# Prompt scores of a decoder step: two stacked full-height maps, or two maps in the two row halves

## The chip, the core and the metric

The program runs on one core of a Trainium2 chip. TensorE multiplies (PE; its weight loads are shown as PEld and run beside the products), VectorE (DVE), ScalarE (ACT) and GpSimd (POOL) do the elementwise work, SyncE (SP) issues the DMAs. The metric is the device time of one execution in microseconds (us), as the median of several runs.

## What is computed

One step of a hybrid decoder layer, for a prompt of 1024 tokens and 8 sample tokens, model width 1024. One projection of h feeds differential attention (4 heads, two maps of 64 channels each, values of 128), a short gated convolution and a chunk-mixing branch; the branches are projected, gated, merged, projected again and normalised. The change concerns the prompt's attention alone:

```python
def block(args):                      # 128 queries at a time
    q_blk, i = args
    s = jnp.einsum('bqhmd,bkhmd->bhmqk', q_blk, k).astype(jnp.float32) * ATT_SCALE
    q_pos = i * Q_BLOCK + jnp.arange(Q_BLOCK)
    mask = key_pos[None, :] <= q_pos[:, None]
    p = jax.nn.softmax(jnp.where(mask, s, -jnp.inf), axis=-1)
    a = p[:, :, 0] - lam * p[:, :, 1]
    return jnp.einsum('bhqk,bkhd->bqhd', a.astype(v.dtype), v)
```

m is the map: each head has two score matrices, each a product over 64 channels.

## The kernel before

Activations lie transposed, channels on the 128 partitions and 1032 tokens along the rows. Every large product is made of exact parts: an operand is split into a rounded part hi (float32r) and a rest lo (`split`, line 85: ACT copies hi, DVE or POOL subtracts), and `gemm` (line 235) adds hi·hi, hi·lo and lo·hi into one PSUM tile `ps_z` of 344 columns: eight chunks of 128 channels, so 24 products for each of the three units of tokens. The program is written in a fixed order. Twice in a unit, after 12 of its 24 products and at its end, `gemm` calls `tick` (line 101), which lets every active side stream (a Python generator) emit its next piece. Each engine runs its instructions in the order in which they were emitted.

The prompt attention of a head is such a side stream (`attention`, line 384). Its plan (lines 496 to 512) gives the tick of each step: block i of 128 queries starts at `start[i]`, scores of map 0 at that tick, of map 1 at the next, then `scale`, `combine`, the transposes and `av`. One head's attention is thus spread over ticks that lie between projection products of the next chunks (`conv_chunk`, the next head's Q, K, V).

For the scores, `evac_q` (line 332) and `evac_k` (line 349) prepare stacked operands of 128 rows. Q0 holds map 0's queries as hi in rows 0 to 63 and lo in rows 64 to 127, Q1 the same for map 1 with hi below. KA holds K's hi part twice, KB its lo part twice, one pair for each map. Two products of full height, KA and KB against the same Q, then give (hi + lo)·(hi + lo) of one map (`scores_map`, lines 429 and 430). The block's keys are nk = 128 (i + 1) columns; from 640 on they are cut into two slices of nk/2. DVE adds the mask and takes the row maximum out of PSUM (line 432), then ACT takes the exponential (line 437). Score tiles come from the pool PX of five PSUM tiles (`xtile`), `ps_z` and `av` from PZ, which has three.

Of the kernel before, what the change touches and what calls it, by code (L numbers as in the profile page):

```python
# [8 lines left out]
F32 = mybir.dt.float32  # L9
F32R = mybir.dt.float32r  # L10
I32 = mybir.dt.int32
AF = mybir.ActivationFunctionType
ALU = mybir.AluOpType
# [3 lines left out]
P = 128  # L17
D = 1024
KD = D // P
NP = 1024  # L20
# [10 lines left out]
SCALE = DK ** -0.5  # L31
# [33 lines left out]
def step_kernel(ctx, tc, cT, sm, sn, lamb, xT, x_p, x_s, ada, adag, bgate, w_in, w_br, w_out, lnb,  # L65
# [12 lines left out]
    S = Slots(spool, NS)  # L78

    pe, act, dve, pool, sp = nc.tensor, nc.scalar, nc.vector, nc.gpsimd, nc.sync  # L80

    def mm(out, lhsT, rhs, start, stop, **kw):
        pe.matmul(out, lhsT=lhsT, rhs=rhs, start=start, stop=stop, **kw)  # L83

    def split(hi, lo, src, eng=None):
        act.copy(hi, src)  # L86
        (eng or dve).tensor_tensor(lo, src, hi, ALU.subtract)  # L87
# [4 lines left out]
    def xtile(name, shape=(P, 512)):  # L92
        return px.tile(list(shape), F32, tag="x", name=name)

    def mtile(name, w):
        return mpool.tile([P, w], F32, tag=f"m{w}", name=name, bufs=12 if w == 2 else 4 if w < 16 else 2)
# [51 lines left out]
    vS = cpool.tile([P, H, NB], F32, name="vS")  # L148
    pt = cpool.tile([1, NB * PAGES], I32, name="pt")

# [1 line left out]
    wseq = []  # L152

    def want(kind, c):
# [22 lines left out]
    first = {c: [S.new(f"w0{x}{c}", F32R) for x in "hl"] for c in (C_Q, C_K, C_V)}  # L177
# [73 lines left out]
                w_split()  # L251
            tick()

# [1 line left out]
    xk, adr = {}, {}  # L255

    def load_ada(k):
# [68 lines left out]
        hh.append(a)  # L326
        hl.append(b)

# [1 line left out]
    st = {}  # L330

    def evac_q(h):
        q0 = S.new(f"Q0_{h}", F32R)
        q1 = S.new(f"Q1_{h}", F32R)
        st["Q", h] = (q0, q1)

        def f(u, a, b, ps):
            b2 = min(b, NP)
            n = b2 - a
            if n:  # L340
                act.copy(q0[0:64, a:b2], ps[0:64, :n])
                dve.tensor_tensor(q0[64:128, a:b2], ps[0:64, :n], q0[0:64, a:b2], ALU.subtract)
                act.copy(q1[64:128, a:b2], ps[64:128, :n])
                dve.tensor_tensor(q1[0:64, a:b2], ps[64:128, :n], q1[64:128, a:b2], ALU.subtract)
            if u == 2:
                dve.tensor_copy(qS[:, h, :], ps[:, n:n + NB])
        return f

    def evac_k(h):
        kf = S.new(f"kf{h}")  # L350

        def f(u, a, b, ps):
            act.copy(kf[:, a:b], ps)
            if u < 2:
                return
            later.append(lambda: sp.dma_start(out=kT_o[h], in_=kf))
            ka0, ka1, kb0, kb1 = (S.new(f"{n}_{h}", F32R) for n in ("KA0", "KA1", "KB0", "KB1"))
            st["K", h] = (ka0, ka1, kb0, kb1)
            pool.tensor_copy(kS[:, h, :], kf[:, NP:T])
            f0, f1 = kf[0:64, :NP], kf[64:128, :NP]  # L360
            dve.tensor_copy(ka0[0:64, :NP], f0)
            act.copy(ka0[64:128, :NP], f0)
            dve.tensor_tensor(kb0[0:64, :NP], f0, ka0[0:64, :NP], ALU.subtract)
            act.copy(kb0[64:128, :NP], kb0[0:64, :NP].bitcast(F32))
            dve.tensor_copy(ka1[64:128, :NP], f1)
            act.copy(ka1[0:64, :NP], f1)
            dve.tensor_tensor(kb1[64:128, :NP], f1, ka1[64:128, :NP], ALU.subtract)
            act.copy(kb1[0:64, :NP], kb1[64:128, :NP].bitcast(F32))
            S.free()
        return f  # L370

# [12 lines left out]
    def attention(h):  # L384
# [6 lines left out]
        mask = S.new(f"mask{h}")  # L391
# [3 lines left out]
        Q, K = st["Q", h], st["K", h]  # L395
        oacc[h] = S.new(f"o{h}")
        E, aT, V = {}, {}, {}

        tmp = {}

        def scores(i, m):
            nk = (i + 1) * P
            if m:
                e, mx, nb, su, rc = tmp.pop(i)
                scores_map(i, 1, nk, e, mx, nb, su)
                tmp[i] = (e, su, rc)
                if i == 7:
                    S.free(7)
                return
            if nk <= 512:  # L410
                t = S.new(f"E{h}_{i}", F32, (P, 2, 512))
                e = [t[:, 0, :nk], t[:, 1, :nk]]
            else:
                e = [S.new(f"E{h}_{i}_{m}")[:, :nk] for m in range(2)]
            mx = mtile(f"mx{h}_{i}", 4)
            nb = mtile(f"nb{h}_{i}", 2)
            su = mtile(f"su{h}_{i}", 2)
            rc = mtile(f"rc{h}_{i}", 2)
            tmp[i] = (e, mx, nb, su, rc)
            scores_map(i, 0, nk, e, mx, nb, su)  # L420

        def scores_map(i, m, nk, e, mx, nb, su):
            g = 1 if nk <= 512 else 2
            w = nk // g
            qq = Q[m][:, i * P:(i + 1) * P]
            for j in range(g):
                ps = xtile(f"s{h}_{i}_{m}_{j}")
                c = slice(j * w, (j + 1) * w)
                mm(ps[:, :w], qq, K[m][:, c], True, False)
                mm(ps[:, :w], qq, K[2 + m][:, c], False, True)  # L430
                m0 = 1024 - nk + j * w
                dve.tensor_tensor_reduce(
                    e[m][:, c], ps[:, :w], mask[:, m0:m0 + w], 1.0,
                    mx[:, 2 * m:2 * m + 1] if j else -3.0e38, ALU.add, ALU.max,
                    mx[:, 2 * m + j:2 * m + j + 1])
            dve.tensor_scalar(nb[:, m:m + 1], mx[:, 2 * m + g - 1:2 * m + g], -SCALE, None, ALU.mult)  # L436
            act.activation(e[m], e[m], AF.Exp, bias=nb[:, m:m + 1], scale=SCALE,  # L437
                           accum_out=su[:, m:m + 1])

        def scale(i):  # L440
            e, su, rc = tmp[i]
# [62 lines left out]
        for i, t in enumerate(start):  # L504
            at(t, scores, i, 0)
            at(t + 1, scores, i, 1)
            at(t + 2, scale, i)
            at(t + 3, combine, i)
            at(t + (7 if i > 2 else 6), trans, i, 0)
            if i >= 4:  # L510
                at(t + 8, trans, i, 1)
# [5 lines left out]
            yield  # L517
        S.free(2)

# [1 line left out]
    yb = {}  # L521

    def conv_chunk(h):
# [47 lines left out]
        gemm("z", C_GC + h, hh, hl, e_gc)  # L571
        gemm("z", C_CB + h, hh, hl, e_cb)

# [1 line left out]
    lt = S.new("lt")  # L575

    def startup():
# [41 lines left out]
        for i, c in enumerate(cs):  # L619
            for k in range(KD):  # L620
                for x, w in enumerate(first[c]):
                    mm(small[0:16, i * P:(i + 1) * P], hs[:, 16 * k:16 * k + 16],
                       w[:, k * P:(k + 1) * P], k == 0 and x == 0, k == KD - 1 and x == 1,
                       skip_group_check=True)
        evs = [f(0) for f in (evac_q, evac_k, evac_v)]
        for c, f in zip(cs, evs):
            for u, (a, b) in enumerate(cut):
# [27 lines left out]
        dve.tensor_scalar(gsub, c2("subg"), 1.0 - LAM0, None, ALU.mult)  # L655
        S.free()

# [1 line left out]
    dec = {}  # L659
    vmax = [0]  # L660

# [185 lines left out]
    for h in range(H):  # L847
        if h:
            gemm("z", C_Q + h, hh, hl, evac_q(h))
            gemm("z", C_K + h, hh, hl, evac_k(h))  # L850
        active.append(attention(h))
        if h == H - 1:
            dec_g = decode(active[0])
            active.append(dec_g)
        if h:
            gemm("z", C_V + h, hh, hl, evac_v(h))
        conv_chunk(h)
    later.append(lambda: sp.dma_start(out=conv_o, in_=convo))

# [1 line left out]
    merged = {}  # L861

    def branch_parts(n, res, gap=0):
# [45 lines left out]
    lo_eng[0] = dve  # L909
    merge(1, True)  # L910

# [1 line left out]
    cvT = {}  # L913

    def evac_cv(g):
# [132 lines left out]

    merge(2, False)

# [1 line left out]
    sq = []  # L1052
    row = mpool.tile([P, H + 1 + NB], F32R, tag="row", name="row", bufs=1)
    dve.tensor_copy(row[:, 0:H], ident[:, 0:P:32])
# [110 lines left out]
    S.free(16)  # L1165
    drain(ag)

# [1 line left out]

    mh, ml = {}, {}  # L1170
    for d in range(KD):
# [41 lines left out]
    for i, n in enumerate(order):  # L1213
# [3 lines left out]
        r = S.new(f"r{n}")  # L1217
# [3 lines left out]
        for f, (a, b) in enumerate(zip(cuts, cuts[1:])):  # L1221
            ps = pz.tile([P, 512], F32, tag="z", name=f"out{n}_{f}")[:, :b - a]
            c = slice(a, b)
            rc = r[0:rows, c]
# [25 lines left out]
        if last:  # L1250
            nb = sd[0:rows, 1:2]
            dve.scalar_tensor_tensor(nb, mu, -1.0, rstd, ALU.mult, ALU.mult)
            rc = r[:, 720:1024]
# [3 lines left out]
        for a, b in ((0, 360), (360, 720)) if last else ((0, 512), (512, 1024)):  # L1257
            rc = r[0:rows, a:b]
# [98 lines left out]
```

## Time and profile before

| what | value |
|---|---|
| runs | 1199.52 us median of 3 (1199.45 to 1200.81) |
| profiled execution, from first to last instruction | span 1197.8 us |
| PE busy | 1180.9 us, 99% of the span |
| DVE, ACT, POOL busy | 640.4, 356.3, 381.8 us |
| granted TensorE clock, mean | 0.998 |

The profile gives no other time of the profiled execution than its span; it is one execution, and the runs are others of the same program. Busy times of different engines overlap. A matmul's length in the profile includes the way through the array, so lengths of successive products overlap as well, and the distance from one start to the next says more than a length.

### The profile page before, as it was taken

To read this page: it belongs to the slowest core of one execution; us is meant where nothing else is said; L and a number is where in the kernel's file an instruction comes from. 1 tells how busy PE (TensorE), PEld (TensorE's weight loads), DVE (VectorE), ACT (ScalarE), POOL (GpSimd) and SP (SyncE) were. 2 spreads that over 40 slices of the span, in tenths; PEclk is the share of its full clock that TensorE was granted. 3 is DMA by queue.
4 is the path that set the end of the run, shared out by engine and by line. 5 is a ranking of instruction groups with operands and counts; after the bars stand their busy time and mean duration, and the time that the engine had idled before them with its cause. 6 is when DMAs were issued, how large, how long until landed. Compare 5 with 4: busy or idle time off the path is not lost.

```text
span 1197.8 us, 20253 instructions
## 1 busy us (share of the span) xinstructions
PE 1180.9 (99%) x7599; PEld 1097.3 (92%) x7599; DVE 640.4 (53%) x1190; ACT 356.3 (30%) x709; POOL 381.8 (32%) x304
## 2 busy tenths in 40 slices
PE   7999999999999999999999999999999999999997
PEld 5799999999999999999999999888887899997785
DVE  5656547536625655777776775111211451197766
ACT  3344454343444342121224223111012232343000
POOL 2123222322322406999980001211211222254000
PEclk9999999999999999999999999999999999999999
DMA  9411110111111116777852234666674111133231
GB/s 358 184 63 37 49 59 29 43 71 37 36 53 63 36 46 208 248 249 234 259 186 65 75 106 140 230 216 223 215 244 158 54 44 45 46 119 120 89 106 53
DMA packets 73300, 146.62 MB, mean 122 GB/s; under 512 B 8409, under 2 KB 9306, under 8 KB 73202
## 3 DMA queue, kind: packets, MB, share of 16 engines
q1 hardware_dynamic: 73202, 145.34, 36.3%
q8 instruction: 59, 0.97, 0.3%
q14 instruction: 39, 0.32, 0.1%
HBM read 136.80 MB, written 8.51 MB: 121 GB/s over the span
## 4 chain that ended last, share of the span: by engine, by line
PE 95%; DVE 3%; DMA 1%; issue 0%; SPq 0%; POOL 0%; ACT 0%
PE ps_z L83 62%; PE ps_b L83 8%; PE out L83 8%; PE acc L83 3%; PE s L83 3%; PE dacc L83 3%; PE av L83 2%; PE t L461 1%; DVE wol L87 1%; DVE ml L1178 1%; DMA ada<-in_ada 1%; PE pa L83 1%; DVE wl L87 1%; PE mix L83 1%; PE cvt L952 0%
## 5 line engine op out<-in xcount | busy, mean ns | idle before, releaser
L83 PE MATMUL ps_z<-hh,wh 128*128 128x344 f32 x1560 | 509.3, 326 | 0.0
L83 PE MATMUL ps_z<-hh,wl 128*128 128x344 f32 x1560 | 498.8, 320 | 0.0
L83 PE MATMUL ps_z<-hl,wh 128*128 128x344 f32 x1560 | 498.3, 319 | 0.0
L83 PEld LDWEIGHTS ps_z<-hh,wh 128*128 128x128 f32 x1560 | 293.3, 188 | 25.8 <-issue 20.2
L83 PEld LDWEIGHTS ps_z<-hl,wh 128*128 128x128 f32 x1560 | 293.6, 188 | 1.5 <-issue 0.2
L83 PEld LDWEIGHTS ps_z<-hh,wl 128*128 128x128 f32 x1560 | 293.1, 188 | 0.2 <-DVE wl L87 0.2
L87 POOL TENSOR_TENSOR wl<-wr,wh 128x512 fp32r<-128x512 f32 x72 | 99.3, 1381 | 265.4 <-ACT wh L86 236.2
L723 POOL TENSOR_TENSOR kp<-kp,QB 128x1024 f32<-128x1024 f32 x64 | 162.0, 2563 | 12.3 <-DMA kp<-in_cache_k 11.4
L87 DVE TENSOR_TENSOR wl<-wr,wh 128x512 fp32r<-128x512 f32 x82 | 85.6, 1044 | 50.3 <-ACT wh L86 44.8
L710 DVE TENSOR_REDUCE Sdec<-kp 128x16 f32<-128x1024 f32 x64 | 77.4, 1213 | 37.8 <-POOL kp L723 37.8
L885 POOL TENSOR_TENSOR mg<-mg,sg 128x344 f32<-128x344 f32 x24 | 28.3, 1180 | 213.6 <-DVE sg L884 213.6
L83 PE MATMUL ps_b<-yh,wh 128*128 128x344 f32 x288 | 94.3, 328 | 0.4
L86 ACT CAST wh<-wr 128x512 fp32r<-128x512 f32 x154 | 93.2, 615 | 0.2
L83 PE MATMUL ps_b<-yl,wh 128*128 128x344 f32 x288 | 92.1, 320 | 0.0
L83 PE MATMUL ps_b<-yh,wl 128*128 128x344 f32 x288 | 92.1, 320 | 0.0
L901 ACT ACTIVATE sg<-ps_z 128x344 f32<-128x344 f32 x48 | 22.0, 458 | 213.3 <-PE ps_z L83 193.3
L437 ACT ACTIVATE E<-E,nb 128x128 f32<-128x128 f32 (+7 forms) x64 | 49.8, 777 | 112.3 <-DVE nb L436 107.0
L83 PEld LDWEIGHTS ps_b<-yh,wh 128*128 128x128 f32 x288 | 54.1, 188 | 11.5 <-issue 5.2
L884 DVE SCALAR_TENSOR_TENSOR sg<-sg,ps_b 128x344 f32<-128x344 f32 x24 | 12.3, 513 | 92.3 <-PE ps_b L83 89.1
L83 PEld LDWEIGHTS ps_b<-yl,wh 128*128 128x128 f32 x288 | 54.2, 188 | 0.1
L83 PEld LDWEIGHTS ps_b<-yh,wl 128*128 128x128 f32 x288 | 54.2, 188 | 0.0
L83 PE MATMUL out<-woh,ml 128*128 128x512 f32 (+1 forms) x136 | 51.9, 382 | 0.0
(285 smaller groups left out, 1518.2 us busy)
## 6 DMA issues: line engine op xcount, KB each, us to landing
wr<-in_w_in SPq DMA_DIRECT2D x136, 256.0 KB, 2.7
kp<-in_cache_k SPq DMA_DIRECT2D x128, 256.0 KB, 3.5
vp<-in_cache_v SPq DMA_DIRECT2D x128, 256.0 KB, 3.6
ada<-in_ada SPq DMA_DIRECT2D x16, 512.0 KB, 8.1
wr<-in_w_br SPq DMA_DIRECT2D x24, 256.0 KB, 2.6
xT<-in_xT SPq DMA_DIRECT2D x8, 516.0 KB, 9.7
adag<-in_adag SPq DMA_DIRECT2D x8, 512.0 KB, 5.7
wr<-in_w_out SPq DMA_DIRECT2D x16, 256.0 KB, 2.6
```

Of the source, the lines that this page charges most:

```text
L83: pe.matmul(out, lhsT=lhsT, rhs=rhs, start=start, stop=stop, **kw)
L86: act.copy(hi, src)
L87: (eng or dve).tensor_tensor(lo, src, hi, ALU.subtract)
L437: act.activation(e[m], e[m], AF.Exp, bias=nb[:, m:m + 1], scale=SCALE, accum_out=su[:, m:m + 1])
L461: pe.transpose(ps[:, kb - lo, :], E[i][:, kb * P:(kb + 1) * P], ident)
L710: dve.reduce_sum(Sx[:, b, 2 * j:2 * j + 2, :], tiles.pop(i).rearrange("p e (a d) -> p e a d", d=DK), axis=AX.X)
L723: pool.tensor_tensor(t, t, q, ALU.mult)
L884: dve.scalar_tensor_tensor(sg[u], sg[u], 1.0, ps, ALU.add, ALU.mult)
L885: pool.tensor_tensor(merged[d][:, a:b], merged[d][:, a:b], sg[u], ALU.add)
L901: act.activation(sg[u], ps, AF.Tanh, scale=0.5)
L1178: dve.scalar_tensor_tensor(ml[d][:, a:b], m, 0.5, mh[d][:, a:b].bitcast(F32), ALU.mult, ALU.subtract)
```

## The change

`evac_q` and `evac_k` no longer stack: for each head there is one pair Qh, Ql and one pair Kh, Kl, 128 rows each, where rows 0 to 63 are map 0 and rows 64 to 127 map 1. `scores(i, j)` now does column slice j of both maps: for each map three products of 64 rows, hi·hi, lo·hi and hi·lo (lo·lo is left out), map 0 in the upper rows of the array and map 1 in the lower, alternating, each map into a PSUM tile of its own. Blocks 0 to 3 have one slice and emit everything at their first tick; blocks 4 to 7 emit slice 0 of both maps at the first tick and slice 1, with both exponentials, at the second. The two K tiles that fall away give two buffers of the pool S back.

```diff
@@ -326,22 +326,19 @@
     st = {}
 
     def evac_q(h):
-        q0 = S.new(f"Q0_{h}", F32R)
-        q1 = S.new(f"Q1_{h}", F32R)
-        st["Q", h] = (q0, q1)
+        qh = S.new(f"Qh_{h}", F32R)
+        ql = S.new(f"Ql_{h}", F32R)
+        st["Q", h] = (qh, ql)
 
         def f(u, a, b, ps):
             b2 = min(b, NP)
             n = b2 - a
             if n:
-                act.copy(q0[0:64, a:b2], ps[0:64, :n])
-                dve.tensor_tensor(q0[64:128, a:b2], ps[0:64, :n], q0[0:64, a:b2], ALU.subtract)
-                act.copy(q1[64:128, a:b2], ps[64:128, :n])
-                dve.tensor_tensor(q1[0:64, a:b2], ps[64:128, :n], q1[64:128, a:b2], ALU.subtract)
+                split(qh[:, a:b2], ql[:, a:b2], ps[:, :n])
             if u == 2:
                 dve.tensor_copy(qS[:, h, :], ps[:, n:n + NB])
         return f
@@ -354,18 +351,10 @@
             if u < 2:
                 return
             later.append(lambda: sp.dma_start(out=kT_o[h], in_=kf))
-            ka0, ka1, kb0, kb1 = (S.new(f"{n}_{h}", F32R) for n in ("KA0", "KA1", "KB0", "KB1"))
-            st["K", h] = (ka0, ka1, kb0, kb1)
+            kh, kl = S.new(f"Kh_{h}", F32R), S.new(f"Kl_{h}", F32R)
+            st["K", h] = (kh, kl)
             pool.tensor_copy(kS[:, h, :], kf[:, NP:T])
-            f0, f1 = kf[0:64, :NP], kf[64:128, :NP]
-            dve.tensor_copy(ka0[0:64, :NP], f0)
-            act.copy(ka0[64:128, :NP], f0)
-            dve.tensor_tensor(kb0[0:64, :NP], f0, ka0[0:64, :NP], ALU.subtract)
-            act.copy(kb0[64:128, :NP], kb0[0:64, :NP].bitcast(F32))
-            dve.tensor_copy(ka1[64:128, :NP], f1)
-            act.copy(ka1[0:64, :NP], f1)
-            dve.tensor_tensor(kb1[64:128, :NP], f1, ka1[64:128, :NP], ALU.subtract)
-            act.copy(kb1[0:64, :NP], kb1[64:128, :NP].bitcast(F32))
+            split(kh[:, :NP], kl[:, :NP], kf[:, :NP])
             S.free()
         return f
 
@@ -398,44 +387,41 @@
 
         tmp = {}
 
-        def scores(i, m):
+        def scores(i, j):
             nk = (i + 1) * P
-            if m:
-                e, mx, nb, su, rc = tmp.pop(i)
-                scores_map(i, 1, nk, e, mx, nb, su)
+            g = 1 if nk <= 512 else 2
+            w = nk // g
+            if j == 0:
+                if g == 1:
+                    t = S.new(f"E{h}_{i}", F32, (P, 2, 512))
+                    e = [t[:, 0, :nk], t[:, 1, :nk]]
+                else:
+                    e = [S.new(f"E{h}_{i}_{m}")[:, :nk] for m in range(2)]
+                tmp[i] = (e, mtile(f"mx{h}_{i}", 4), mtile(f"nb{h}_{i}", 2), mtile(f"su{h}_{i}", 2),
+                          mtile(f"rc{h}_{i}", 2))
+            if j >= g:
+                return
+            e, mx, nb, su, rc = tmp[i]
+            c = slice(j * w, (j + 1) * w)
+            ps = [xtile(f"s{h}_{i}_{m}_{j}") for m in range(2)]
+            for x, y in ((0, 0), (0, 1), (1, 0)):
+                for m in range(2):
+                    r = slice(64 * m, 64 * m + 64)
+                    mm(ps[m][:, :w], Q[x][r, i * P:(i + 1) * P], K[y][r, c], x + y == 0, x == 1)
+            m0 = 1024 - nk + j * w
+            for m in range(2):
+                dve.tensor_tensor_reduce(
+                    e[m][:, c], ps[m][:, :w], mask[:, m0:m0 + w], 1.0,
+                    mx[:, 2 * m:2 * m + 1] if j else -3.0e38, ALU.add, ALU.max,
+                    mx[:, 2 * m + j:2 * m + j + 1])
+                if j == g - 1:
+                    dve.tensor_scalar(nb[:, m:m + 1], mx[:, 2 * m + j:2 * m + j + 1], -SCALE, None, ALU.mult)
+                    act.activation(e[m], e[m], AF.Exp, bias=nb[:, m:m + 1], scale=SCALE,
+                                   accum_out=su[:, m:m + 1])
+            if j == g - 1:
                 tmp[i] = (e, su, rc)
                 if i == 7:
-                    S.free(7)
-                return
-            if nk <= 512:
-                t = S.new(f"E{h}_{i}", F32, (P, 2, 512))
-                e = [t[:, 0, :nk], t[:, 1, :nk]]
-            else:
-                e = [S.new(f"E{h}_{i}_{m}")[:, :nk] for m in range(2)]
-            mx = mtile(f"mx{h}_{i}", 4)
-            nb = mtile(f"nb{h}_{i}", 2)
-            su = mtile(f"su{h}_{i}", 2)
-            rc = mtile(f"rc{h}_{i}", 2)
-            tmp[i] = (e, mx, nb, su, rc)
-            scores_map(i, 0, nk, e, mx, nb, su)
-
-        def scores_map(i, m, nk, e, mx, nb, su):
-            g = 1 if nk <= 512 else 2
-            w = nk // g
-            qq = Q[m][:, i * P:(i + 1) * P]
-            for j in range(g):
-                ps = xtile(f"s{h}_{i}_{m}_{j}")
-                c = slice(j * w, (j + 1) * w)
-                mm(ps[:, :w], qq, K[m][:, c], True, False)
-                mm(ps[:, :w], qq, K[2 + m][:, c], False, True)
-                m0 = 1024 - nk + j * w
-                dve.tensor_tensor_reduce(
-                    e[m][:, c], ps[:, :w], mask[:, m0:m0 + w], 1.0,
-                    mx[:, 2 * m:2 * m + 1] if j else -3.0e38, ALU.add, ALU.max,
-                    mx[:, 2 * m + j:2 * m + j + 1])
-            dve.tensor_scalar(nb[:, m:m + 1], mx[:, 2 * m + g - 1:2 * m + g], -SCALE, None, ALU.mult)
-            act.activation(e[m], e[m], AF.Exp, bias=nb[:, m:m + 1], scale=SCALE,
-                           accum_out=su[:, m:m + 1])
+                    S.free(5)
 
         def scale(i):
             e, su, rc = tmp[i]
```

The rest of the diff takes out comment lines.

On PE, head 0, block 0, of the kernel before (s_0_0 and s_0_1 are the score tiles of map 0 and 1, ps_z a projection; 12 products of it stand between the two ticks):

```order
L83 MATMUL ps_z_2_829<-hh_606,wl_516 128x344
L83 MATMUL s_0_0_0_867<-KA_0_776,Q_0_719 128x128
L83 MATMUL s_0_0_0_867<-KB_0_778,Q_0_719 128x128
L83 MATMUL ps_z_0_873<-hh_172,wh_647 128x344
...
L83 MATMUL ps_z_0_873<-hh_359,wl_648 128x344
L83 MATMUL s_0_1_0_886<-KA_0_777,Q_0_720 128x128
L83 MATMUL s_0_1_0_886<-KB_0_779,Q_0_720 128x128
L83 MATMUL ps_z_0_873<-hh_426,wh_764 128x344
```

The same place after:

```order
L83 MATMUL ps_z_2_817<-hh_606,wl_516 128x344
L83 MATMUL s_0_0_0_855<-Kh_772,Qh_719 128x128
L83 MATMUL s_0_1_0_856<-Kh_772,Qh_719 128x128
L83 MATMUL s_0_0_0_855<-Kl_773,Qh_719 128x128
L83 MATMUL s_0_1_0_856<-Kl_773,Qh_719 128x128
L83 MATMUL s_0_0_0_855<-Kh_772,Ql_720 128x128
L83 MATMUL s_0_1_0_856<-Kh_772,Ql_720 128x128
L83 MATMUL ps_z_0_869<-hh_172,wh_647 128x344
```

Map 1 has moved up to map 0's tick, and four products of 128 rows in two pairs have become six of 64 rows in one run, map 0 and map 1 by turns.

On PE, head 0, block 4, before (the last number of a name but one is the slice):

```order
L83 MATMUL ps_z_2_1157<-hh_359,wl_909 128x344
L83 MATMUL s_4_0_0_1176<-KA_0_776,Q_0_719 128x320
L83 MATMUL s_4_0_0_1176<-KB_0_778,Q_0_719 128x320
L83 MATMUL s_4_0_1_1180<-KA_0_776,Q_0_719 128x320
L83 MATMUL s_4_0_1_1180<-KB_0_778,Q_0_719 128x320
L83 MATMUL ps_z_2_1157<-hh_426,wh_964 128x344
...
L83 MATMUL ps_z_2_1157<-hh_606,wl_965 128x344
L83 MATMUL s_4_1_0_1202<-KA_0_777,Q_0_720 128x320
L83 MATMUL s_4_1_0_1202<-KB_0_779,Q_0_720 128x320
L83 MATMUL s_4_1_1_1206<-KA_0_777,Q_0_720 128x320
L83 MATMUL s_4_1_1_1206<-KB_0_779,Q_0_720 128x320
L83 MATMUL ps_z_0_1212<-hh_172,wh_1085 128x344
```

And after, where the third part shows the start of the second tick's run:

```order
L83 MATMUL ps_z_2_1153<-hh_359,wl_899 128x344
L83 MATMUL s_4_0_0_1172<-Kh_772,Qh_719 128x320
L83 MATMUL s_4_1_0_1173<-Kh_772,Qh_719 128x320
L83 MATMUL s_4_0_0_1172<-Kl_773,Qh_719 128x320
L83 MATMUL s_4_1_0_1173<-Kl_773,Qh_719 128x320
L83 MATMUL s_4_0_0_1172<-Kh_772,Ql_720 128x320
L83 MATMUL s_4_1_0_1173<-Kh_772,Ql_720 128x320
L83 MATMUL ps_z_2_1153<-hh_426,wh_956 128x344
...
L83 MATMUL ps_z_2_1153<-hh_606,wl_957 128x344
L83 MATMUL s_4_0_1_1198<-Kh_772,Qh_719 128x320
L83 MATMUL s_4_1_1_1199<-Kh_772,Qh_719 128x320
```

Each tick of block 4 had both slices of one map in four products; it now has one slice of both maps in six.

## Rows read from the trace of the kernel before

**Rows 1.** The page: span, PE's busy time and share, the chain by engine and line

```profile
span 1197.8 us, 20253 instructions
...
PE 1180.9 (99%) x7599; PEld 1097.3 (92%) x7599; DVE 640.4 (53%) x1190; ACT 356.3 (30%) x709; POOL 381.8 (32%) x304
...
PE 95%; DVE 3%; DMA 1%; issue 0%; SPq 0%; POOL 0%; ACT 0%
PE ps_z L83 62%; PE ps_b L83 8%; PE out L83 8%; PE acc L83 3%; PE s L83 3%; PE dacc L83 3%; PE av L83 2%; PE t L461 1%; DVE wol L87 1%; DVE ml L1178 1%; DMA ada<-in_ada 1%; PE pa L83 1%; DVE wl L87 1%; PE mix L83 1%; PE cvt L952 0%
```

**Rows 2.** Busy time by stretches: us, then PE, PEld, DVE, ACT, POOL, clock, DMA

```profile
75.00:175.00 100.00, 100.00 (x661) 98.98 (x660) 57.12 (x159) 46.25 (x105) 30.89 (x34) 1.00 0.14 48
175.00:275.00 100.00, 100.00 (x659) 99.11 (x658) 50.93 (x130) 42.12 (x90) 29.88 (x31) 1.00 0.14 48
```

**Rows 3.** All waits of PE: us in total, times, longest

```profile
PE pa L83 <- DMA ada<-in_ada: 6.9, 3, 5.9
PE pb L83 <- ACT part L300: 0.5, 1, 0.5
```

**Rows 4.** Chain from 70 to 425 us by line; groups of instructions, the scores

```profile
by line: PE ps_z L83 78.4%; PE s L83 9.6%; PE av L83 6.9%; PE t L461 4.1%; PE vt L476 1.0%
...
L83 PE MATMUL s<-KA,Q 128*128 128x384 f32 (+5 forms) x96 | 32.9, 344 | 0.0
```

**Rows 5.** Pieces of the chain in order of time: start, us, what

```profile
78.27 0.23 PE s L83 x2
...
78.51 1.88 PE ps_z L83 x12
...
172.23 0.47 PE s L83 x2
...
181.72 0.58 PE s L83 x4
...
204.35 0.81 PE s L83 x4
```

**Rows 6.** Timeline around mxB: start us, us, engine, line, operation, out<-in, shape

```profile
646.97 0.31 PE L83 MATMUL ps_z<-hh,wl 128*128 128x344 f32 x1
...
647.21 0.29 PEld L83 LDWEIGHTS mxB<-dm,ones 64*128 64x128 f32 x2 [0.21 <-issue]
...
647.57 0.19 PEld L83 LDWEIGHTS ps_z<-hh,wh 128*128 128x128 f32 x1
...
647.68 0.19 PEld L83 LDWEIGHTS ps_z<-hl,wh 128*128 128x128 f32 x1
...
647.84 0.32 PE L83 MATMUL ps_z<-hl,wh 128*128 128x344 f32 x1
```

**Rows 7.** Timeline around zsT

```profile
65.20 0.32 PE L83 MATMUL ps_z<-hh,wl 128*128 128x344 f32 x1
...
65.45 0.74 PEld L83 LDWEIGHTS zsT<-sel,zs 16*128 16x128 f32 x6 [0.22 <-issue]
...
66.21 0.19 PEld L83 LDWEIGHTS ps_z<-hh,wh 128*128 128x128 f32 x1
```

**Rows 8.** Timeline around the first dacc

```profile
680.86 0.32 PE L83 MATMUL ps_z<-hh,wl 128*128 128x344 f32 x1
...
681.11 0.12 PEld L83 LDWEIGHTS dacc<-vp,Sdec 128*8 128x8 f32 x8 [0.22 <-issue]
...
682.08 0.19 PEld L83 LDWEIGHTS ps_z<-hh,wh 128*128 128x128 f32 x1 [0.86 <-issue]
```

**Rows 9.** Timeline around rsum, plain float32 at full height

```profile
655.25 1.02 PE L83 MATMUL rsum<-wm,ones 128*128 128x512 f32 x2
...
656.11 0.19 PEld L83 LDWEIGHTS ps_z<-hl,wh 128*128 128x128 f32 x1 [0.24 <-issue]
```

**Rows 10.** Groups on ACT: a copy of K from 50 to 75 us, the exponentials

```profile
L364 ACT CAST KB<-KB 64x1024 fp32r<-64x1024 f32 x1 | 1.0, 1046 | 1.7 <-DVE KB L363 1.7
...
L437 ACT ACTIVATE E<-E,nb 128x128 f32<-128x128 f32 (+7 forms) x64 | 49.8, 777 | 112.3 <-DVE nb L436 107.0
```


## The prediction

> **What bounds the kernel now.** I read the page first, then the busy time by stretches, then the waits, then the chain of work inside the attention stage, and last the timeline around a few places. The page says that TensorE (PE) is busy 99% of a span of 1197.8 us and holds 95% of the chain that ended last [rows 1]. An average hides stages, so the next question is whether the stage that the change touches has the same limit. It does: from 75 to 275 us PE is busy 100.00 of every 100.00 us at a granted clock of 1.00, while DVE and ACT are busy about half of the time [rows 2]. In the whole run PE waited for another engine or a DMA only four times, 7.4 us in all, every time at the conditioning products (pa, pb) of the startup [rows 3]. So in the prompt attention nothing but PE's own stream sets the pace: a microsecond put into or taken out of that stream is a microsecond of the end, and work moved on DVE, ACT or POOL costs nothing while PE never waits for it.
>
> How large is the piece that changes? In the chain from 70 to 425 us, the stretch of all four heads' attention, PE's score products (s) hold 9.6% [rows 4], that is 0.096 x 355 = 34.1 us. A product's length in the profile overlaps its successor's, so 32.9 us for 96 products [rows 4] is no cost; what counts is the distance from start to start, the pitch. It stands in the chain's pieces: 0.23/2 = 0.115 us at 256 columns, 0.47/2 = 0.235 at 512, 0.58/4 = 0.145 at 320, 0.81/4 = 0.20 at 448, and for the projections of 344 columns 1.88/12 = 0.157 [rows 5].
>
> **The change part by part.** Products: a block before takes four full-height products for each slice of columns (two maps, each a hi and a lo part of K against Q stacked over 128 rows). After, it takes six of 64 rows, alternating between the upper and the lower row half. If the two halves run abreast, six half products are three pitches. One pitch in four goes: 34.1/4 = 8.5 us saved.
>
> Switches: before, all 192 score products are full height like the projections around them. After, they stand in bursts of six between full-height products. Blocks 0 to 3 have one burst each and blocks 4 to 7 two, since they are cut in two column slices on successive ticks: 4 + 8 = 12 a head, 48 in all. What does PE pay to go from full height to a part of the rows and back? The trace has a few such places. The nearest one is mxB, whose two products use 64 rows by 128 columns [rows 6]. In the steady stream a weight load begins as the product before it starts. Here the last full product starts at 646.97 and the first 64-row load only at 647.21, 0.24 later. The row says that the load path stood idle 0.21 us for "issue", so nothing in the program held it. zsT, 16 rows high, shows 65.20 to 65.45 = 0.25 [rows 7], and dacc, cut by columns, 680.86 to 681.11 = 0.25 [rows 8]. The first tile product then follows after its load: six loads of zsT span 0.74 us, the last lasting 0.19, so (0.74 - 0.19)/5 = 0.11 each [rows 7]. From the last full product to the first half product that is 0.24 + 0.11 = 0.35 against a pitch of 0.157: 0.19 lost on the way in.
>
> On the way out: two passes of 512 columns of a plain float32 product at full height take 655.25 to 656.11 = 0.86 us, for the second load behind them begins as the first projection product does [rows 9]. dacc's eight passes, four strips abreast, take the same two pass times, 0.86, yet from its first load to the first full-height load there are 682.08 - 681.11 = 0.97 us [rows 8]: some 0.10 for the last product to drain, the rest for a tiny first load. Then the full-height load itself lies open, 647.57 to 647.68 = 0.11 [rows 6]. The way out loses 0.10 + 0.11 = 0.21. Both ways: 0.40 us a burst.
>
> Bounds: zsT as a whole, 65.20 to 66.21 and a load of 0.11, is 1.12 us; less one pitch and six loads of 0.11 that leaves 0.30 [rows 7], and mxB likewise 0.71 - 0.157 - 0.22 = 0.33 [rows 6]. There the products have 8 and 64 columns, shorter than a load, and the load swallows part of the drain; the scores have 128 to 512 columns, as dacc has, so I take 0.40. The upper end is 0.51, if the lower half's first load also waits for the upper half's. So 48 x 0.40 = 19.2 us, between 48 x 0.30 = 14.4 and 48 x 0.51 = 24.5.
>
> Whether two row halves run abreast no row shows. dacc's four column strips do run abreast, by the passes above: eight passes in the time of two [rows 8, 9]. From both sides: three pitches a slice (minus 8.5 us) or six (plus 17.0). I take three, by that nearest row.
>
> The Trainium skill, "TensorE: Matmul & The Clock Gate", Part 3 (Measured speedup vs the span model), has four row tiles at 3.07 times the speed of one; no run here shows it. Taken as an estimate at 3.07/4 = 0.77 of the ideal, three pairs would cost 3.9 pitches, the 8.5 us of saving would shrink to 0.9, and the time would be 1218. The same skill, "TensorEngine Tiling (Array Packing)", Restrictions and Gotchas, says that two row tiles can't use the same PSUM bank at once; here the two maps write separate tiles of the x pool, so it wouldn't bite.
>
> Evacuation of Q and K: for K, eight instructions over 64 rows become two over 128, for Q four become two per unit; one of K's copies on ACT is 1.05 us [rows 10]. Less work on DVE and ACT, hidden behind a PE that is busy throughout [rows 2]: 0 us. K can't arrive later than now, since its row of four DVE and four ACT instructions becomes one of each, and earlier gains nothing where PE doesn't wait [rows 3].
>
> Order on the other engines: in blocks 0 to 3 both maps' scores come in one tick, needing two x tiles at once as blocks 4 to 7 do already. In blocks 4 to 7 map 0's exponential moves one tick later and stands right ahead of map 1's. DVE's reciprocal of the sums, two ticks after the start, then waits for one exponential more (0.78 us on average [rows 10]), with z evacuations and the next splits queued behind it. PE would feel that only after the three z buffers, 24 products of 0.157 = 3.8 us apart, are used up: 0 us. If that cover were gone it would cost at most 16 blocks x 0.78 = 12 us. SP's and POOL's instructions keep their ticks.
>
> Sum against the profiled execution: 1197.8 - 8.5 + 19.2 = 1208.5 us of span. The median of the runs, 1199.5, lies 1.7 above that span; with the same 1.7 the forecast is **1210.2 us**.
>
> **Rivals.** (a) The halves run abreast but their weight loads don't. Then a pair can't be shorter than two loads, 0.22 us. That binds below 512 columns: per head 0.105 at 128 and 256 columns each, 0.045 at three slices of 384, 0.075 at two of 320, 0.02 at two of 448, together 0.535, times three pairs and four heads 6.4 us, and 48 x 0.11 = 5.3 for the second half's first load: 1222. For it: the zsT loads do follow each other at 0.11 [rows 7]. Against: those share one set of rows, and dacc's eight loads fit in 0.12 [rows 8], though they are only 8 columns wide.
>
> (b) The halves take turns. Six pitches for four, 1197.8 + 17.0 + 19.2 + 1.7 = 1236. For it: strips by columns write different output partitions, while both halves write all 128, which no row here covers. Against: eight passes in the time of two [rows 8, 9].
>
> (c) Not slower: the switch is nearly free here. Every row on it belongs to plain float32 products, and a float32r load of 64 rows might slip in beneath the running product as full-height loads do. Without the switch the saving stands alone: 1197.8 - 8.5 + 1.7 = 1191. The point from which it decides is a switch of 8.5/48 = 0.18 us. Against: the three places show 0.24 to 0.25 before the first load, whether rows or columns are cut, 16, 64 or 128 rows high [rows 6 to 8].
>
> (d) The switch costs about 0.18, the two terms cancel, and the time stays at 1199.5. No row says so; it is the gap between (c) and the forecast.
>
> **How the numbers follow.** Forecast 0.62, (a) 0.12, (b) 0.10, (c) 0.10, (d) 0.06. The forecast's own range runs with the switch from 0.30 (1205) to 0.51 (1215.5). To leave out no more than 2 in 10 the range takes in (a) above and most of (d) below: 1199 to 1223; (b) and (c) stay outside. Within 0.2% means within 2.4 us of 1199.5, about what a measurement of this kernel can tell from no change: (d), 0.06. Faster is (c) and a little of (d), 0.11; slower is the rest, 0.83.
>
> **What would show it.** Each score burst should begin with a load idle for some 0.2 us on "issue", 48 times in all, and end with a full-height load 0.1 after the last product has streamed. Within a burst the two halves' products should start within a few hundredths of each other, and the pairs one pitch apart: pairs 0.22 apart whatever the width mean (a), single products one pitch apart mean (b). PE should stay at 100.00 of 100.00 us; the stretch of attention should be 10 us longer and all after it shifted by that. The forecast is wrong if PE begins to wait for DVE (the exponentials' order), or if the first load of a burst begins with the product before it, as in (c).

## The result, and the profile after

| | median of the runs | ratio to before, 95% interval |
|---|---|---|
| before | 1199.49 us (4 runs) | |
| after | 1209.64 us (4 runs) | 1.0085 [1.0071, 1.0099] |

The changed kernel is slower by 10.2 us; 10.7 were forecast. Its page, with the lines that answer to [rows 1]:

```profile
span 1207.7 us, 20350 instructions
...
PE 1189.9 (99%) x7695; PEld 1087.0 (90%) x7695; DVE 617.8 (51%) x1167; ACT 339.1 (28%) x686; POOL 379.1 (31%) x304
...
PE 95%; DVE 3%; DMA 1%; issue 0%; SPq 0%; POOL 0%; ACT 0%
```

The span has grown by 9.9 us and PE's busy time by 9.0, while DVE and ACT have lost 22.6 and 17.2 us of work. That work bought nothing, as PE was and is the bound. Busy time by stretches, as in [rows 2], and all waits of PE, as in [rows 3]:

```profile
75.00:175.00 100.00, 100.00 (x670) 93.36 (x670) 51.88 (x152) 39.84 (x94) 29.08 (x33) 1.00 0.13 44
175.00:275.00 100.00, 100.00 (x665) 94.16 (x664) 44.67 (x121) 36.55 (x81) 27.60 (x31) 1.00 0.14 48
```

```profile
PE pa L83 <- DMA ada<-in_ada: 7.9, 3, 5.5
PE pb L83 <- ACT part L300: 0.5, 1, 0.5
```

PE is "busy" 100.00 of 100.00 us and waits for nobody in the attention, yet it gets less done: a busy PE is not a PE at its peak. What has dropped is the weight loads' busy time, from 99 us in each 100 to 93 and 94. Who held the loads up is in the waits of PEld, the longest first (us in total, times, longest):

```profile
PEld ps_z L83 <- issue: 29.4, 58, 0.9
PEld s L83 <- issue: 8.8, 41, 0.2
```

Before, the 192 loads for the scores had 1.0 us of idle load path ahead of them in all. Now it is idle 41 times on "issue", 0.21 us each. Of the other 7 of the 48 runs (unbroken rows of half products), three stood idle as long and are put down to a DVE semaphore that came last, and four, which start behind a product of `av`, show only 0.07. The same idle times ahead of a projection's load went from 26 to 58; some more are put down to an ACT instruction that came last, as the one of 0.37 below.

One run of six at 512 columns, head 1, block 3, from the timeline after (start us, us, engine, line, operation, out<-in, height and columns):

```profile
175.43 0.31 PE L83 MATMUL ps_z<-hh,wl 128*128 128x344 f32 x1
175.67 0.19 PEld L83 LDWEIGHTS s<-Kh,Qh 64*128 64x128 f32 x2 [0.21 <-issue]
175.68 0.50 PE L83 MATMUL s<-Kh,Qh 64*128 64x512 f32 x2
175.78 0.19 PEld L83 LDWEIGHTS s<-Kl,Qh 64*128 64x128 f32 x2
176.01 0.40 PE L83 MATMUL s<-Kl,Qh 64*128 64x512 f32 x2
176.02 0.19 PEld L83 LDWEIGHTS s<-Kh,Ql 64*128 64x128 f32 x2
176.25 0.40 PE L83 MATMUL s<-Kh,Ql 64*128 64x512 f32 x2
176.58 0.19 PEld L83 LDWEIGHTS ps_z<-hh,wh 128*128 128x128 f32 x1 [0.37 <-ACT cc L515]
...
176.68 0.19 PEld L83 LDWEIGHTS ps_z<-hl,wh 128*128 128x128 f32 x1
```

Both halves' loads and products stand in one line each (x2), and a line of two loads is as long as one load, 0.19: they start together. The pairs start 0.23 to 0.24 apart, one pitch of 512 columns. In: last full product 175.43, first half load 175.67, next load (and with it the first pair) 175.78, so 0.35. Out: the last pair starts at 176.25 and its columns take 0.235, the full load begins 0.09 later at 176.58, and the first full product 0.11 later still at 176.68, as the second load shows. From full product to full product 1.25 us; less its own pitch of 0.157 and three of 0.235 that leaves 0.39 for the switch. At 320 columns it is about the same:

```profile
99.79 0.32 PE L83 MATMUL ps_z<-hh,wl 128*128 128x344 f32 x1
...
100.79 0.19 PEld L83 LDWEIGHTS ps_z<-hl,wh 128*128 128x128 f32 x1
```

99.79 to 100.79 = 1.00, less 0.157 and three of 0.147: 0.40. At 128 columns, where the pairs follow each other at the 0.11 of their loads, it is less:

```profile
74.00 0.32 PE L83 MATMUL ps_z<-hh,wl 128*128 128x344 f32 x1
74.25 0.19 PEld L83 LDWEIGHTS s<-Kh,Qh 64*128 64x128 f32 x2 [0.21 <-issue]
...
74.36 0.19 PEld L83 LDWEIGHTS s<-Kl,Qh 64*128 64x128 f32 x2
...
74.47 0.19 PEld L83 LDWEIGHTS s<-Kh,Ql 64*128 64x128 f32 x2
...
74.73 0.19 PEld L83 LDWEIGHTS ps_z<-hh,wh 128*128 128x128 f32 x1
...
74.84 0.19 PEld L83 LDWEIGHTS ps_z<-hl,wh 128*128 128x128 f32 x1
```

74.00 to 74.84 = 0.84, less 0.157 and three loads of 0.11: 0.35.

The other runs agree. Worked out in this way from the starts in the trace, the 43 of the 48 that follow a projection product give 0.39 to 0.40 on average at each width from 256 to 512 columns and 0.35 at 128. The pairs themselves start 0.147, 0.175 and 0.204 us apart at 320, 384 and 448 columns, where the full-height score products before stood 0.147, 0.176 and 0.203 apart: a pair costs what one full-height product costs.

### The profile page after: what moved, and what is told of

Read it like the earlier page. It is cut to its first block, busy times and chain, and to the rows that moved or that the text cites. A ratio compares the mean times of both kernels' runs of the same rounds, so it can differ in the third digit from the quotient of the medians.

```text
span 1207.7 us, 20350 instructions
## 1 busy us (share of the span) xinstructions
PE 1189.9 (99%) x7695; PEld 1087.0 (90%) x7695; DVE 617.8 (51%) x1167; ACT 339.1 (28%) x686; POOL 379.1 (31%) x304
## 4 chain that ended last, share of the span: by engine, by line
PE 95%; DVE 3%; DMA 1%; issue 0%; SPq 0%; POOL 0%; ACT 0%
PE ps_z L83 63%; PE ps_b L83 8%; PE out L83 8%; PE acc L83 3%; PE s L83 3%; PE dacc L83 3%; PE av L83 2%; PE t L447 1%; DVE wol L87 1%; DMA ada<-in_ada 1%; DVE ml L1164 1%; PE pa L83 1%; DVE wl L87 1%; PE mix L83 1%; PE cvt L938 0%
## 5 line engine op out<-in xcount | busy, mean ns | idle before, releaser
L83 PE MATMUL ps_z<-hh,wh 128*128 128x344 f32 x1560 | 514.5, 330 | 0.0
L87 DVE TENSOR_TENSOR aT_l<-t,aT_h 128x512 fp32r<-128x512 f32 (+3 forms) x48 | 26.7, 557 | 49.8 <-ACT aT_h L86 49.7
```

## The experiments

Theory: each run of half products pays a fixed price of 0.35 to 0.40 us for the two switches, and three pairs abreast save one pitch of four. Rivals: the loss lies in the half products, in halves that take turns, or in the new order on DVE, ACT and the x tiles. Seven kernels tell them apart. A run of products, below, is an unbroken row of half products between full-height ones.

| kernel | runs of half products | median us | ratio to before, 95% interval |
|---|---|---|---|
| changed kernel | 48 | 1209.64 | 1.0085 [1.0071, 1.0099] |
| one run per block | 32 | 1203.85 | 1.0035 [1.0022, 1.0047] |
| six runs a head | 24 | 1200.90 | 1.0010 [0.9994, 1.0025] |
| map by map | 48 | 1209.72 | 1.0085 [1.0069, 1.0100] |
| full height with zeros | 0 | 1216.64 | 1.0143 [1.0128, 1.0159] |
| upper rows only | 64 | 1223.69 | 1.0199 [1.0183, 1.0214] |
| stacked, new order | 0 | 1199.36 | 0.9990 [0.9977, 1.0003] |
| one pair | 48 | 1191.49 | 0.9925 [0.9899, 0.9951] |

Each was timed beside the kernel before: 1199.33 us for those named one run per block, map by map, full height and upper rows, 1199.67 for the other three. The ratios are worked out from all runs and differ a little from those of the medians.

**One run per block.** Fewer switches with the same products:

```diff
-            if j >= g:
+            if j:
                 return
-            e, mx, nb, su, rc = tmp[i]
+            for j in range(g):
+                slice_scores(i, j, g, w, nk)
+
+        def slice_scores(i, j, g, w, nk):
+            e, mx, nb, su, rc = tmp[i]
```

> The changed kernel, but blocks 4 to 7 do both column slices in their first tick: twelve half-height products in one run instead of two runs of six. The products are the same; 32 runs stand between full-height products instead of 48. Switch theory (each run pays about 0.39 us for going to the row halves and back, the products themselves save 8.5 us): 16 x 0.39 = 6.2 us less than the changed kernel, 1209.6 - 6.2 = 1203.4 us. Rival, the loss lies in the half products themselves (loads, PSUM, halves that hinder each other): no change, 1209.6. Rival, it lies in the new order (two x tiles at once, exponentials late): no better, rather worse, since four x tiles are now needed at once.

Measured 1203.85, 5.8 less than the changed kernel, where 6.2 were expected: 0.36 us for each of the 16 runs that went. A run of twelve at 320 columns in its timeline:

```profile
100.65 0.32 PE L83 MATMUL ps_z<-hh,wl 128*128 128x344 f32 x1
100.90 0.19 PEld L83 LDWEIGHTS s<-Kh,Qh 64*128 64x128 f32 x2 [0.22 <-issue]
...
101.30 0.32 PE L83 MATMUL s<-Kh,Ql 64*128 64x320 f32 x2
...
101.45 0.31 PE L83 MATMUL s<-Kh,Qh 64*128 64x320 f32 x2
...
101.98 0.19 PEld L83 LDWEIGHTS ps_z<-hh,wh 128*128 128x128 f32 x1 [0.19 <-issue]
...
102.09 0.19 PEld L83 LDWEIGHTS ps_z<-hl,wh 128*128 128x128 f32 x1
```

Between the third and the fourth pair, where the second slice begins, there is nothing but a pitch of 0.15. The price stands at both ends alone: the run holds 100.65 to 102.09 = 1.44, two runs of six hold 2 x 1.00, and the 0.56 between them are a projection's pitch of 0.157 and one price of 0.40.

**Six runs a head.** Blocks 0 and 1, and 2 and 3, are moved together as well:

```diff
         for i, t in enumerate(start):
-            at(t, scores, i, 0)
-            at(t + 1, scores, i, 1)
+            at(start[i - 1] if i in (1, 3) else t, scores, i, 0)
```

> As the kernel with one run per block, and blocks 0 and 1, and 2 and 3, share a run too: 6 runs a head, 24 in all, same products. Switch theory: the time lies on the line through 48 and 32 runs, 1209.6 - 24 x 0.39 = 1200.3 us (by the two points measured, 0.36 a run: 1200.9). If the first runs to merge held the dearer switches, or four x tiles taken at once make PE wait: above that. Below 1199.5 it can't come by this theory, as 24 x 0.36 is still more than the 8.5 us that the products save.

Measured 1200.90. With 48, 32 and 24 runs the times are 1209.64, 1203.85 and 1200.90: 0.36 and 0.37 us a run. They lie on a line within the intervals. (Taken against the kernel before that was timed beside each, the losses are 10.15, 4.52 and 1.23 us: 0.35 and 0.41 a run, 0.37 over both steps.) The kernel with 24 runs can't be told from the kernel before, and it is not faster: at 24 switches the price still takes up the whole saving. The four x tiles taken at once in one tick made PE wait nowhere in the attention.

**Upper rows only.** The kernel before with its 64 runs of two or four products, each read at 64 rows:

```diff
-            qq = Q[m][:, i * P:(i + 1) * P]
+            qq = Q[m][0:64, i * P:(i + 1) * P]
...
-                mm(ps[:, :w], qq, K[m][:, c], True, False)
-                mm(ps[:, :w], qq, K[2 + m][:, c], False, True)
+                mm(ps[:, :w], qq, K[m][0:64, c], True, False)
+                mm(ps[:, :w], qq, K[2 + m][0:64, c], False, True)
```

> The kernel before, its four products a slice and its order untouched, but each product reads only the upper 64 rows of its operands (this leaves out map 0's lo part of Q and uses map 1's lo part alone). So nothing runs abreast and the number of products is that of before; only the height is that of the changed kernel. The scores stand in 16 runs a head, 64 in all. Switch theory: 64 x 0.39 = 25 us more, 1224.5 us (with 0.30: 1218.7). Rival without a price on the switch: 1199.5.

Measured 1223.69, 24.4 us more for 64 runs: 0.38 each. Nothing else differs from the kernel before, neither order nor evacuation nor number of products. The timeline at 320 columns:

```profile
101.86 0.32 PE L83 MATMUL ps_z<-hh,wl 128*128 128x344 f32 x1
102.11 0.18 PEld L83 LDWEIGHTS s<-KA,Q 64*128 64x128 f32 x1 [0.22 <-issue]
...
102.36 0.30 PE L83 MATMUL s<-KB,Q 64*128 64x320 f32 x1
102.36 0.18 PEld L83 LDWEIGHTS s<-KA,Q 64*128 64x128 f32 x1
102.50 0.31 PE L83 MATMUL s<-KA,Q 64*128 64x320 f32 x1
...
102.88 0.19 PEld L83 LDWEIGHTS ps_z<-hh,wh 128*128 128x128 f32 x1 [0.20 <-issue]
...
102.99 0.19 PEld L83 LDWEIGHTS ps_z<-hl,wh 128*128 128x128 f32 x1
```

Here all products use one half, each line is a single product (x1), and they follow each other at 0.14 to 0.15: one pitch. The switch is again 102.99 - 101.86 - 0.157 - 4 x 0.145 = 0.39.

**Full height with zeros.** Six products without a switch and without halves:

```diff
-                    r = slice(64 * m, 64 * m + 64)
-                    mm(ps[m][:, :w], Q[x][r, i * P:(i + 1) * P], K[y][r, c], x + y == 0, x == 1)
+                    mm(ps[m][:, :w], Q[m][x][:, i * P:(i + 1) * P], K[y][:, c], x + y == 0, x == 1)
```

(`evac_q` writes four tiles instead of two, one map's rows of each, and POOL clears the other rows.)

> The changed kernel with the same six products a slice, each at full height: the queries of each map lie in tiles of their own whose other 64 rows are zero. Order, exponentials and PSUM tiles stay as in the changed kernel; POOL clears four half tiles a head. No switch, no halves abreast. Switch theory: six pitches instead of before's four, 1199.5 + 2 x 8.5 = 1216.5 us, that is 7 above the changed kernel. Rival, the halves take turns and the switch is cheap: equal to the changed kernel, 1209.6. Rival, the new order costs something by itself: above 1216.5 by that.

Measured 1216.64, by the switch theory 1216.5. Two pitches more than before cost 17.3 us, which sizes the pitch sum at 8.65. In its chain (start, us, what) six products of 320 columns hold

```profile
99.57 0.89 PE s L83 x6
```

0.89 us, six pitches, without any idle load around them; in the changed kernel the same piece is

```profile
100.11 0.64 PE s L83 x6
```

0.64, of which the pairs take 0.44. So the row halves beat six full-height products by 7.0 us (1209.64 against 1216.64); what they lose to is the stacking, which needs only four.

**Stacked, in the new order.** The changed kernel's `scores(i, j)` with the operands and products of before:

```diff
-            for x, y in ((0, 0), (0, 1), (1, 0)):
-                for m in range(2):
-                    r = slice(64 * m, 64 * m + 64)
-                    mm(ps[m][:, :w], Q[x][r, i * P:(i + 1) * P], K[y][r, c], x + y == 0, x == 1)
+            for m in range(2):
+                qq = Q[m][:, i * P:(i + 1) * P]
+                mm(ps[m][:, :w], qq, K[m][:, c], True, False)
+                mm(ps[m][:, :w], qq, K[2 + m][:, c], False, True)
```

> The changed kernel's order (both maps of a column slice in one tick, exponentials at the last slice) with the stacked operands and the four full-height products of before. So only the products differ from the changed kernel, and only the order from the one before. Switch theory: the order is worth nothing, since PE never waits on DVE or ACT there: 1199.5 us. Rival, part of the 10 us belongs to the order (exponentials one tick later, two x tiles at once): above 1201.9, up to 1209.6.

Measured 1199.36 against 1199.67: no difference that can be told. The interval reaches from 2.8 us less to 0.4 us more, so the order of maps and slices, the later exponentials and the two x tiles at once don't account for the 10 us.

**One pair.** Only hi by hi:

```diff
-            for x, y in ((0, 0), (0, 1), (1, 0)):
-                for m in range(2):
+            for m in range(2):
...
-                    mm(ps[m][:, :w], Q[x][r, i * P:(i + 1) * P], K[y][r, c], x + y == 0, x == 1)
+                mm(ps[m][:, :w], Q[0][r, i * P:(i + 1) * P], K[0][r, c], True, True)
```

> The changed kernel with only the hi by hi pair of the three (this leaves out the lo parts of the scores). The 48 runs and their switches stay. If a pair costs one pitch of a full-height product, two pairs less are 2 x 8.5 = 17 us: 1192.6 us. If the halves took turns in truth, 34 us less: 1175.6. If the weight loads set the pace of a pair (0.22 us below 512 columns), 17 + 2/3 x 6.4 = 21 us less: 1188.

Measured 1191.49, 18.2 less than the changed kernel for 96 pairs. That is two pitch sums of 9.1 where full height gave 8.65; with an interval of 3 us on either side it can't tell these apart, but it excludes halves that take turns. Loads that set the pace, at 1188, lie just inside the interval; it is the rows that exclude them, since the loads of a pair start together and the pairs at 320 columns follow each other at 0.147, below two loads of 0.11. The timeline at 512 columns:

```profile
169.68 0.32 PE L83 MATMUL ps_z<-hh,wl 128*128 128x344 f32 x1
169.92 0.19 PEld L83 LDWEIGHTS s<-Kh,Qh 64*128 64x128 f32 x2 [0.21 <-issue]
...
170.35 0.19 PEld L83 LDWEIGHTS ps_z<-hh,wh 128*128 128x128 f32 x1 [0.24 <-issue]
...
170.46 0.19 PEld L83 LDWEIGHTS ps_z<-hl,wh 128*128 128x128 f32 x1
```

0.78 from full product to full product instead of 1.25: two pairs are 0.47, twice the pitch of 0.235, and 0.78 - 0.157 - 0.235 = 0.39 is the switch once more.

**Map by map.** The six products in another order:

```diff
-            for x, y in ((0, 0), (0, 1), (1, 0)):
-                for m in range(2):
+            for m in range(2):
+                for x, y in ((0, 0), (0, 1), (1, 0)):
                     r = slice(64 * m, 64 * m + 64)
```

> The changed kernel with the six products of a run in another order: map 0's three, then map 1's three, instead of by turns. Same products, same number of switches. If the halves run abreast only where neighbours in the queue use different halves, just the third of map 0 and the first of map 1 overlap: five pitches a slice instead of three, two more, 2 x 8.5 = 17 us: 1226.6 us. If PE reorders so far that both halves stay busy: 1209.6. If the halves never ran abreast (and the profile's starts mislead): 1209.6 too, but then the full-height kernel of six products would have to be no slower either.

Measured 1209.72, as by turns, and 16.9 below the 1226.6 of queue order. What that says is told under the last heading.

## Why the prediction was right

- **The bound.** PE alone sets the time of this stage: 100.00 of 100.00 us before and after, no wait of PE in it, and the new order alone costs nothing that can be told (1199.36 against 1199.67). The lighter evacuation, 22.6 us of DVE and 17.2 of ACT, gave nothing back, as costed.
- **The saving.** That two row halves run abreast was carried over from dacc's column strips without a row of its own. The nearest row was the right one to go by, but it was another shape, and that it carried over is in part luck. It holds: pairs start one pitch apart at every width, six products of full height cost 17.3 us more than four, and a run of 320 columns takes 0.44 for six half products where full height takes 0.89. Rivals (a) and (b) are out, the weight loads of the halves run abreast too.
- **The switch.** It was built from three places with other shapes and put at 0.40 between 0.30 and 0.51. The trace after shows 0.39 to 0.40 from 256 to 512 columns and 0.35 at 128; the slope over 48, 32 and 24 runs gives 0.36 to 0.37, the kernel at 64 rows 0.38. Its parts are right too: at 512 columns 0.35 from the last full product to the first pair, as forecast, and 0.09 and 0.11 on the way out where 0.10 and 0.11 were forecast. Rival (c), a nearly free switch for float32r, is out: the first half load of a run stands 0.24 to 0.26 us behind the last projection product (0.20 behind a product of `av` or a transpose), as it did in [rows 6 to 8].
- **Sizes.** By the starts in the trace, 44 runs at 0.395 and four at 0.35 are 18.8 us against the 19.2 forecast, and a pitch for each of the 48 slices is 8.6 us against the 8.5 forecast (8.65 by the kernel with six full-height products). 18.8 - 8.6 = 10.2 us, the loss measured. Half of the 0.4 us between forecast and trace comes from the 128-column runs, four of the 48, which were costed like the wide ones. The run times alone would put the switches at 17.3 to 18.2 us (0.36 to 0.38 a run), and so the saving at 7.1 to 8.0; with intervals of over a microsecond they don't contradict the trace.
- **The Trainium skill's 3.07.** The Trainium skill, "TensorE: Matmul & The Clock Gate", Part 3 (Measured speedup vs the span model), gives four row tiles 3.07 times the speed of one. As an estimate at 0.77 of the ideal that made 1218. For two halves the pairs here ran at the pitch of one full-height product (0.147 us at 320 columns in both), so nothing was lost in the pairs themselves; four tiles were not run.

## What to carry to other kernels

Packing two small products into the row halves pays only where a run of them saves more than the way in and out, here 0.35 to 0.40 us: against six full-height products it did, against four it didn't. Count the runs, not the products, and multiply. Before splitting an operand over the array, look whether stacking hi and lo parts over all rows does it in full-height products that need no switch. A price for an operation that the trace doesn't contain can come from small places far off that share its mechanism, if their own work is taken out first and their shape is compared with the new one.

## What the hardware showed that was not expected

The order in which the two halves' products are queued didn't matter: emitted as three of the upper half and then three of the lower they took 1209.72 us, by turns 1209.64. Had the lower half's first product waited for its place in the queue, two pitches a slice would have shown as 17 us. The timeline of that kernel at 512 columns:

```profile
174.83 0.31 PE L83 MATMUL ps_z<-hh,wl 128*128 128x344 f32 x1
175.07 0.19 PEld L83 LDWEIGHTS s<-Kh,Qh 64*128 64x128 f32 x2 [0.21 <-issue]
175.08 0.51 PE L83 MATMUL s<-Kh,Qh 64*128 64x512 f32 x2
...
175.42 0.41 PE L83 MATMUL s<-Kl,Qh 64*128 64x512 f32 x2
...
175.65 0.40 PE L83 MATMUL s<-Kh,Ql 64*128 64x512 f32 x2
...
176.09 0.19 PEld L83 LDWEIGHTS ps_z<-hl,wh 128*128 128x128 f32 x1
```

174.83 to 176.09 = 1.26, against 1.25 by turns: the first products of both halves start together although two others of the upper half stand between them in the program. So the lower half's first product, load included, went ahead of two products of the upper half that were emitted before it and start at 175.42 and 175.65. The section on the kernel before says that each engine runs its instructions in the order in which they were emitted; on PE that doesn't hold for products of different row halves. How far ahead this reaches, with more than three queued on one half, was not tried.
